# Experts that start with one pair's gather, and half of the memory's products behind the first up products

## The chip, the cores and the metric

The kernel runs as one program on 1 core of one Trainium2 chip. The metric is the device time of an execution in microseconds (us). Five engines work side by side: TensorE (PE; its weight loads are PEld), VectorE (DVE), ScalarE (ACT), GpSimd (POOL) and SyncE (SP), which issues most of the DMA transfers.

## The reference

Two blocks run one after the other on 256 tokens of 1024 features, in float32. The change lies in the first block's two layers. Each is an attention mixer, a layer norm and a mixture of 16 experts, of which a token takes two:

```python
scores = sigmoid(h @ router_w)                      # 256 x 16
# the group of four experts with the best sum of two; in it the best two
gates = sel / sum(sel);  dense_gates = one_hot(idx) weighted by gates
for e in range(16):
    a = silu(h @ w_gate[e]) * (h @ w_up[e])         # 1024 -> 512
    y = y + dense_gates[:, e:e+1] * (a @ w_down[e]) # 512 -> 1024
h = layer_norm(ALPHA * h + y)
```

The second block attends to a memory of 256 rows. Its keys and values, `rms_norm(mem) @ mem_wkv` (1024 to 2048 columns), depend on the input alone. The kernel computes them in four pieces of 512 columns, two in each expert stage of the first block, and keeps them in DRAM until the second block.

## The kernel before

**The expert stage.** The kernel doesn't run each expert on all 256 tokens. It counts for every token its place among the at most 64 (CAP) tokens of an expert, writes these places as matrices of ones and zeros (`pm`, one per tile of 128 tokens, tile name `gv`) and gathers the tokens by matmuls with them. Experts run in eight pairs, each expert of a pair on 64 columns of TensorE. Per pair come gate products, up products, silu times up times gate weight (`act`), a transpose (`tr`), down products and the scatter back to the rows of `res`. `gather(g)` (L1273) makes the transposed inputs of two pairs at once, with 256 columns; the pairs' inputs lie in slots m0 and m1.

**Ahead of the experts.** `LayerNorm.tile` (L206) normalises a tile of 128 tokens, transposes it (L560) and copies it (L564, L566); for the second tile it also splits both tiles into a high and a low float32r part (`split`, L491) for the gather. Then come the routing (L1189 to L1232), the counts by matmul (L1237 to L1241), the places (L1248), `gather(0)`, the memory's products of 512 columns (`memory_gemm`, L1709: 16 matmuls, of 1024 x 512 weights in two halves), which the scheduler fits between the others, and the products that bring the gate weights to the places (L1296). A float32 matmul shows as two records on TensorE, a float32r matmul as one.

**What sets the order.** The functions write the instructions in an order; a scheduler then orders each engine by priority and readiness, and `after` ties an instruction behind another on its engine. Each engine runs its list in that fixed order, and an instruction that waits holds up all behind it. PSUM banks come from rings: `mm` has 3, `acca` and `accb` 2 each, `tp` 1. The small tiles `prob` have 2 buffers: the memory's products are scaled into them (L1734) and sent to DRAM by GpSimd's queue (L1736), and `act` (L1324, L1325) takes the same two.

**The weights' stream.** `plan` (L330) lists the weights as units of 1 MB in the order of use. `Stream` loads them strictly in that order on SP's queue (L141), into 7 buffers called stage and 6 called piece; four units of the first pairs (`slots`) go into main slots that are free then (m4, xl, m1, xh). A unit's load is issued when the oldest buffer of its ring has been given back by `release`, which `gate_or_up` and `down` call after every half (2 MB). A unit's index decides the ring.

Of the kernel before, what the change touches and what calls it, by code (L numbers as in the profile page):

```python
# [16 lines left out]
P = 128  # L17
# [6 lines left out]
NSTAGE = 7  # L24
# [174 lines left out]
class LayerNorm:  # L199
# [6 lines left out]
    def tile(self, t):  # L206
        k = self.k
        self.sqrt, self.last = k.ln_full(self.res, t, self.gb)
        if self.plain:
            if t == 0:  # L210
                self.n = k.slot(self.tags[0]).rearrange("p (j n) -> p j n", j=8)
            self.copied = k.plain_t(self.res[:, t, :], t, self.n)
            if t == 0:
                return

            self.hh = k.slot("m5", F32R).rearrange("p (t j f) -> p t j f", t=2, j=8)
            self.hl = k.slot("m2", F32R).rearrange("p (t j f) -> p t j f", t=2, j=8)
            with k.after(self.sqrt, self.last):
                for i in range(2):
                    v = self.res[:, i, :].rearrange("p (f j) -> p j f", j=8)  # L220
                    k.split(v, self.hh[:, i], self.hl[:, i])
        else:
            if t == 0:
                self.hi, self.lo = k.xt(self.tags[0]), k.xt(self.tags[1])
            self.copied = k.x_t(self.res[:, t, :], t, self.hi, self.lo, self.g)
            if t == 0:
                self.half = self.copied
            self.moved = k.moved
# [38 lines left out]
class Kern:  # L267
# [62 lines left out]
    def plan(self):  # L330
        I, ws = self.I, self.ws
        for l in range(2):
# [31 lines left out]
            def mem(c0):  # L364
                for j0 in (0, 4):
                    ws.raw("mem", w_mem[:, j0:j0 + 4, c0:c0 + 512], 4, 512, j0 // 4)

            mem(1024 * l)
            n = 0
            for k in range(9):  # L370
# [3 lines left out]
                if k > 0:  # L374
                    todo += [("down", e, j0) for j0 in (0, 4) for e in (2 * k - 2, 2 * k - 1)]
                for key in todo:
# [3 lines left out]
                    ws.raw(key[0], *w_ap(*key), n % (NSTAGE + NPIECE) % 2)  # L380
                    n += 1
                    if n == NSTAGE + NPIECE - 2:
                        early("down", 1, 0)
                        early("down", 0, 4)
            mem(1024 * l + 512)
# [793 lines left out]
    def moe(self, l, res, ln):  # L1179
# [6 lines left out]
        for t in range(2):  # L1186
            o = p[:, 16 * t:16 * t + 16]
            for j in range(8):
                nc.tensor.matmul(o, n[:, j, t * P:(t + 1) * P], self.rw[:, j, :], start=(j == 0), stop=(j == 7))  # L1189
# [56 lines left out]
        for e0, e1 in ((0, 4), (4, 16)):  # L1246
            for t in range(2):
                at_pm = nc.vector.tensor_tensor(  # L1248
# [3 lines left out]
                    op=OP.is_equal)  # L1252
        pos = self.sm(48, "gpos")
# [35 lines left out]
        gather(0)  # L1289
        self.memory_gemm(l, 0, [self.prob()[:, 0:512] for t in range(2)], {7: [at_pp]})  # L1290

        p = self.tp()
        gsl = self.sm(8, "gsl")
        for pr in range(8):
            for t in range(2):
                nc.tensor.matmul(p[:, 2 * pr:2 * pr + 2], pm[t][:, P * pr:P * pr + P].bitcast(F32),  # L1296
                                 gates[:, 16 * t + 2 * pr:16 * t + 2 * pr + 2], start=(t == 0), stop=(t == 1))
        pv = p[:, 0:16].rearrange("p (a k) -> p a k", k=2)
        for k in range(2):
            nc.vector.tensor_copy(gsl[64 * k:64 * k + 64, :], pv[64 * k:64 * k + 64, :, k])  # L1300
# [71 lines left out]
        for pr in range(9):  # L1372
# [23 lines left out]
            if pr < 8:  # L1396
                ua = gate_or_up("up", pr)
            if pend is not None:
# [310 lines left out]
    def memory_gemm(self, k, b, out, after={}, mid=None, pair=None):  # L1709

        acc = [self.acc(pair), self.acc(pair)]
        x = self.mem_t.rearrange("p (j n) -> p j n", j=8)
        with ExitStack() as order:
            for j in range(8):
# [11 lines left out]
        if not mid:  # L1726
# [548 lines left out]
```

## Time and profile before

| | |
|---|---|
| median of 3 runs | 1941.78 us (1941.69 to 1943.78) |
| the profiled execution | 1940.31 us, of it 1938.5 us from the first to the last instruction |
| mean granted TensorE clock | 0.998 |
| busy share: PE, PEld, DVE, ACT, POOL | 98%, 75%, 58%, 45%, 2% |
| bytes moved by DMA | 453.36 MB, 234 GB/s over the span |
| first layer's experts | about 150 to 407 us |
| second layer's experts | about 532 to 789 us |

The expert stages are the stretches in which the DMA engines move the most, some 425 GB/s; in most of the rest they move 110 to 240 GB/s. Matmul ends are modelled, so a TensorE that is called busy may still be waiting for pieces of a pipeline; gaps and the distance from one start to the next are the better measure. What ended a gap stands in brackets behind a row.

### The profile page before, as it was taken

Reading aid. Unit: us, or ns where it says so; the run is one execution under the profiler, and the core shown is the slowest. Engines: PE = TensorE matmul, PEld = TensorE weight load, DVE = VectorE, ACT = ScalarE, POOL = GpSimd, SP = SyncE. Lnnn points to the kernel's source line nnn. Section 1 sums busy time; section 2 is a strip of 40 time slices with the busy share of each in tenths; the row PEclk is TensorE's granted clock in tenths of the full one; section 3 lists DMA queues with packets and bytes.
Section 4 is the critical chain, followed back from the end, with each engine's and each line's share of the span. In section 5 each row is a group of like instructions: output and inputs, shape, how many; then the busy total and the mean of one; then the engine's idle time right before and its main releaser. Section 6 shows DMA issues by size and latency. Waiting matters only on the chain.

```text
span 1938.5 us, 27919 instructions
## 1 busy us (share of the span) xinstructions
PE 1891.8 (98%) x11029; PEld 1449.2 (75%) x11029; DVE 1117.4 (58%) x2226; ACT 862.8 (45%) x1550; POOL 46.4 (2%) x93
## 2 busy tenths in 40 slices
PE   6999999999999999999999999999999999999999
PEld 6775444378754443799988988899899986788998
DVE  6875122277741223765579857555655568766554
ACT  5662111056521101654477656544644466656443
POOL 1010000000000000000001000000000000000000
PEclk9999999999999999999999999999999999999999
DMA  8568999964679999655553553555555553434550
GB/s 284 174 232 297 399 426 426 423 235 157 236 305 414 425 426 422 235 187 211 181 185 110 175 217 131 194 179 183 195 174 196 195 164 135 152 109 157 192 196 23
DMA packets 175211, 453.36 MB, mean 234 GB/s; under 512 B 10288, under 2 KB 106012, under 8 KB 148316
## 3 DMA queue, kind: packets, MB, share of 16 engines
q1 hardware_dynamic: 171212, 435.53, 60.2%
q0 software_dynamic: 3856, 15.91, 2.4%
q8 instruction: 91, 1.49, 0.3%
q14 instruction: 52, 0.43, 0.1%
HBM read 446.17 MB, written 5.24 MB: 233 GB/s over the span
## 4 chain that ended last, share of the span: by engine, by line
PE 60%; ACT 2%; DMA 2%; DVE 2%; issue 0%; POOL 0%; ACTq 0%; SPq 0%
PE mm L1588 8%; PE mm L1589 8%; PE mm L1587 8%; PE acca L487 5%; PE acca L488 5%; PE accb L486 4%; PE accb L487 4%; PE accb L488 4%; PE acca L486 4%; PE mm L1315 2%; DMA piece<-in_exp_w_down_dram 1%; DMA piece<-in_exp_w_gate_dram 1%; PE mm L1851 1%; PE acca L1348 1%; PE accb L1348 1%; PE mm L545 1%
## 5 line engine op out<-in xcount | busy, mean ns | idle before, releaser
L167 DVE TENSOR_TENSOR piece<-stage,piece 128x1024 fp32r<-128x1024 f32 (+3 forms) x439 | 513.5, 1179 | 238.2 <-ACT piece L166 236.6
L166 ACT ACTIVATE piece<-stage 128x1024 fp32r<-128x1024 f32 (+3 forms) x439 | 444.1, 1022 | 335.8 <-PE mm L1589 198.3
L1315 PE MATMUL mm<-stage,m 128*64 128x512 f32 x528 | 225.1, 595 | 2.4 <-DMA stage<-in_exp_w_gate_dram 2.4
L1315 PE MATMUL mm<-piece,m 128*64 128x512 f32 x480 | 213.4, 595 | 2.6 <-DMA piece<-in_exp_w_gate_dram 2.5
L1588 PE MATMUL mm<-m,piece 128*128 128x256 f32 x736 | 206.6, 281 | 0.0
L1587 PE MATMUL mm<-m,piece 128*128 128x256 f32 x736 | 206.2, 280 | 0.0
L1589 PE MATMUL mm<-m,piece 128*128 128x256 f32 x736 | 206.1, 280 | 0.0
L1587 PE MATMUL mm<-xh,piece 128*128 128x256 f32 x576 | 163.1, 283 | 0.0
L1589 PE MATMUL mm<-xh,piece 128*128 128x256 f32 x576 | 163.0, 283 | 0.0
L1588 PE MATMUL mm<-xl,piece 128*128 128x256 f32 x576 | 162.9, 283 | 0.0
L486 PE MATMUL accb<-piece,m 128*128 128x512 f32 (+1 forms) x364 | 143.2, 394 | 1.4 <-DVE res L1670 0.8
L487 PE MATMUL accb<-piece,m 128*128 128x512 f32 (+1 forms) x364 | 144.4, 397 | 0.0
L488 PE MATMUL accb<-piece,m 128*128 128x512 f32 (+1 forms) x364 | 144.2, 396 | 0.0
L1587 PEld LDWEIGHTS mm<-m,piece 128*128 128x128 f32 x736 | 138.4, 188 | 1.9 <-issue 0.3
L1588 PEld LDWEIGHTS mm<-m,piece 128*128 128x128 f32 x736 | 138.2, 188 | 1.6 <-issue 0.2
L1589 PEld LDWEIGHTS mm<-m,piece 128*128 128x128 f32 x736 | 138.7, 189 | 0.2 <-issue 0.2
L486 PE MATMUL acca<-piece,m 128*128 128x512 f32 (+1 forms) x348 | 137.3, 396 | 0.9 <-ACT m L496 0.8
L487 PE MATMUL acca<-piece,m 128*128 128x512 f32 (+1 forms) x348 | 137.8, 396 | 0.0
L488 PE MATMUL acca<-piece,m 128*128 128x512 f32 (+1 forms) x348 | 137.3, 395 | 0.0
L1315 PEld LDWEIGHTS mm<-stage,m 128*64 128x64 f32 x528 | 67.7, 137 | 82.9 <-issue 74.8
L1587 PEld LDWEIGHTS mm<-xh,piece 128*128 128x128 f32 x576 | 110.4, 192 | 1.3
L1588 PEld LDWEIGHTS mm<-xl,piece 128*128 128x128 f32 x576 | 110.4, 192 | 1.2
(572 smaller groups left out, 3480.2 us busy)
## 6 DMA issues: line engine op xcount, KB each, us to landing
stage<-in_ffn_wi_dram SPq DMA_DIRECT2D x88, 1024.0 KB, 5.1
stage<-in_ffn_wo_dram SPq DMA_DIRECT2D x44, 1024.0 KB, 5.1
stage<-in_exp_w_gate_dram SPq DMA_DIRECT2D x34, 1024.0 KB, 12.5
stage<-in_exp_w_down_dram SPq DMA_DIRECT2D x34, 1024.0 KB, 13.0
stage<-in_exp_w_up_dram SPq DMA_DIRECT2D x32, 1024.0 KB, 13.0
piece<-in_exp_w_gate_dram SPq DMA_DIRECT2D x30, 1024.0 KB, 10.6
piece<-in_exp_w_up_dram SPq DMA_DIRECT2D x30, 1024.0 KB, 11.0
piece<-in_exp_w_down_dram SPq DMA_DIRECT2D x24, 1024.0 KB, 19.5
```

The source lines that it names most:

```text
L166: nc.scalar.activation(wh, src, AF.Copy)
L167: nc.vector.tensor_tensor(wl, src, wh.bitcast(F32), op=OP.subtract)
L486: nc.tensor.matmul(out, ah, bh, start=first, stop=False)
L487: nc.tensor.matmul(out, ah, bl, start=False, stop=False)
L488: self.last_mm = nc.tensor.matmul(out, al, bh, start=False, stop=last)
L545: self.moved = nc.tensor.transpose(p[:, k * P:(k + 1) * P], src[:, 4 * q + k:D:8], self.c["ident"])
L1315: mm = nc.tensor.matmul(o[64 * k:64 * k + 64, :], x[:, j, s:s + CAP], w[k][:, jj, :], start=(j == 0), stop=(j == 7))
L1348: prev[:] = [nc.tensor.matmul(y[nb][64 * k:64 * k + 64, :], x[:, f, 64 * k:64 * k + 64], w[k][:, cc, nb * 512:(nb + 1) * 512], start=(f == ...
L1587: nc.tensor.matmul(out, wh[:, j, :], hi[:, j, :], start=(j == 0), stop=False)
L1588: nc.tensor.matmul(out, wh[:, j, :], lo[:, j, :], start=False, stop=False)
L1589: nc.tensor.matmul(out, wl[:, j, :], hi[:, j, :], start=False, stop=(j == 7))
L1851: nc.tensor.matmul(po[:, k * P:(k + 1) * P], v[:, mc, h * 256 + cc * P:h * 256 + (cc + 1) * P], pt[t][:, (2 * h + mc) * P:(2 * h + mc + 1) ...
```

## The change

It does five things. (1) The places are written for the first pair alone, then for the rest, behind the copies of the first gather. (2) The gather of the first two pairs is cut in two gathers of 128 columns; the second stands behind the first up products. (3) Of the memory's 16 products the first 8 stay ahead of the experts, and the 8 with the second half of the weights stand behind the second pair's gather; so does the product that brings the gate weights to the places. (4) In the stream, the second half of the memory's weights moves behind the first pair's up weights. (5) The split of the second tile into two parts stands behind that tile's copies.

```diff
--- before.py
+++ after.py
@@ -218,7 +218,8 @@
             with k.after(self.sqrt, self.last):
                 for i in range(2):
                     v = self.res[:, i, :].rearrange("p (f j) -> p j f", j=8)
-                    k.split(v, self.hh[:, i], self.hl[:, i])
+                    with k.after(*(self.copied if i else ())):
+                        k.split(v, self.hh[:, i], self.hl[:, i])
         else:
             if t == 0:
                 self.hi, self.lo = k.xt(self.tags[0]), k.xt(self.tags[1])
@@ -361,11 +362,10 @@
             self.plan_rows("w_out", I["w_out"][l].rearrange("(c p) n -> p c n", p=P), 8)
             early("up", 0, 4)
             w_mem = I["mem_wkv_2"].rearrange("(p j) n -> p j n", j=8)
-            def mem(c0):
-                for j0 in (0, 4):
-                    ws.raw("mem", w_mem[:, j0:j0 + 4, c0:c0 + 512], 4, 512, j0 // 4)
-
-            mem(1024 * l)
+            def mem(c0, j0, ring):
+                ws.raw("mem", w_mem[:, j0:j0 + 4, c0:c0 + 512], 4, 512, ring)
+
+            mem(1024 * l, 0, 0)
             n = 0
             for k in range(9):
                 todo = []
@@ -373,16 +373,23 @@
                     todo += [(name, e, j0) for name in ("gate", "up") for j0 in (0, 4) for e in (2 * k, 2 * k + 1)]
                 if k > 0:
                     todo += [("down", e, j0) for j0 in (0, 4) for e in (2 * k - 2, 2 * k - 1)]
+                if k == 0:
+                    todo.append("mem")
                 for key in todo:
                     if key in slots:
                         ws.use(key[0], held[key])
                         continue
-                    ws.raw(key[0], *w_ap(*key), n % (NSTAGE + NPIECE) % 2)
+                    ring = n % (NSTAGE + NPIECE) % 2
+                    if key == "mem":
+                        mem(1024 * l, 4, ring)
+                    else:
+                        ws.raw(key[0], *w_ap(*key), ring)
                     n += 1
-                    if n == NSTAGE + NPIECE - 2:
+                    if n == NSTAGE + NPIECE - 1:
                         early("down", 1, 0)
                         early("down", 0, 4)
-            mem(1024 * l + 512)
+            for j0 in (0, 4):
+                mem(1024 * l + 512, j0, j0 // 4)
 
             if l == 0:
                 w = I["w_in"][1].rearrange("(p j) n -> p j n", j=8)
@@ -1186,7 +1193,7 @@
         for t in range(2):
             o = p[:, 16 * t:16 * t + 16]
             for j in range(8):
-                nc.tensor.matmul(o, n[:, j, t * P:(t + 1) * P], self.rw[:, j, :], start=(j == 0), stop=(j == 7))
+                routed = nc.tensor.matmul(o, n[:, j, t * P:(t + 1) * P], self.rw[:, j, :], start=(j == 0), stop=(j == 7))
         ws.free.append("xh")
         with self.tc.issue_after(ln.sqrt.ins):
             self.table(AF.Sigmoid)
@@ -1243,13 +1250,17 @@
         nc.vector.scalar_tensor_tensor(posx, sel, -FAR, pp[:, 0:32], op0=OP.mult, op1=OP.add)
 
         pm = [self.mp.tile([P, D], F32R, name="gv", tag="gv", bufs=2) for t in range(2)]
-        for e0, e1 in ((0, 4), (4, 16)):
+
+        def places(e0, e1):
             for t in range(2):
-                at_pm = nc.vector.tensor_tensor(
+                at = nc.vector.tensor_tensor(
                     pm[t][:, CAP * e0:CAP * e1].rearrange("p (e n) -> p e n", n=CAP),
                     c["slot"][:, None, 0:CAP].to_broadcast([P, e1 - e0, CAP]),
                     posx[:, 16 * t + e0:16 * t + e1].rearrange("p (e o) -> p e o", o=1).to_broadcast([P, e1 - e0, CAP]),
                     op=OP.is_equal)
+            return at
+
+        at_pm = places(0, 2)
         pos = self.sm(48, "gpos")
         nc.vector.tensor_copy(pos, pp[:, 0:48])
 
@@ -1286,18 +1297,41 @@
                 nc.scalar.activation(x[:, j0, :], p[:, 0:256], AF.Copy)
                 nc.vector.tensor_copy(x[:, j0 + 1, :], p[:, 256:512])
 
-        gather(0)
-        self.memory_gemm(l, 0, [self.prob()[:, 0:512] for t in range(2)], {7: [at_pp]})
-
-        p = self.tp()
+        def gather_pair(q):
+
+            if not xg:
+                xg.append(self.slot("m0").rearrange("p (j n) -> p j n", j=8))
+            x = xg[0][:, :, P * q:P * q + P]
+            for j0 in range(0, 8, 4):
+                p = self.mm()
+                for j in range(j0, j0 + 4):
+                    o = p[:, P * (j - j0):P * (j - j0) + P]
+                    for t in range(2):
+                        m = pm[t][:, P * q:P * q + P]
+                        nc.tensor.matmul(o, hh[:, t, j, :], m, start=(t == 0), stop=False)
+                        nc.tensor.matmul(o, hl[:, t, j, :], m, start=False, stop=(t == 1))
+                p4 = p.rearrange("p (j n) -> p j n", j=4)
+                nc.scalar.activation(x[:, j0:j0 + 2, :], p4[:, 0:2], AF.Copy)
+                at = nc.vector.tensor_copy(x[:, j0 + 2:j0 + 4, :], p4[:, 2:4])
+            return at
+
+        at_x = gather_pair(0)
+        with self.after(at_x):
+            at_pm = places(2, 16)
+        mem_out = [self.prob()[:, 0:512] for t in range(2)]
+        self.memory_gemm(l, 0, mem_out, {2: [routed], 3: [at_pp]}, js=range(4))
         gsl = self.sm(8, "gsl")
-        for pr in range(8):
-            for t in range(2):
-                nc.tensor.matmul(p[:, 2 * pr:2 * pr + 2], pm[t][:, P * pr:P * pr + P].bitcast(F32),
-                                 gates[:, 16 * t + 2 * pr:16 * t + 2 * pr + 2], start=(t == 0), stop=(t == 1))
-        pv = p[:, 0:16].rearrange("p (a k) -> p a k", k=2)
-        for k in range(2):
-            nc.vector.tensor_copy(gsl[64 * k:64 * k + 64, :], pv[64 * k:64 * k + 64, :, k])
+
+        def place_gates():
+
+            p = self.tp()
+            for pr in range(8):
+                for t in range(2):
+                    nc.tensor.matmul(p[:, 2 * pr:2 * pr + 2], pm[t][:, P * pr:P * pr + P].bitcast(F32),
+                                     gates[:, 16 * t + 2 * pr:16 * t + 2 * pr + 2], start=(t == 0), stop=(t == 1))
+            pv = p[:, 0:16].rearrange("p (a k) -> p a k", k=2)
+            for k in range(2):
+                nc.vector.tensor_copy(gsl[64 * k:64 * k + 64, :], pv[64 * k:64 * k + 64, :, k])
 
         act_t, ptr = [], []
 
@@ -1395,6 +1429,11 @@
                     scatter(pr - 2, y)
             if pr < 8:
                 ua = gate_or_up("up", pr)
+            if pr == 0:
+                with self.after(state["up"]):
+                    gather_pair(1)
+                    place_gates()
+                    self.memory_gemm(l, 0, mem_out, js=range(4, 8), acc=self.mem_out[2])
             if pend is not None:
                 y = down(pr - 1, at)
             if pr == 1:
@@ -1706,12 +1745,12 @@
         self.mem_t = self.slot(tag)
         self.nc.gpsimd.dma_start(self.mem_t, self.memT)
 
-    def memory_gemm(self, k, b, out, after={}, mid=None, pair=None):
-
-        acc = [self.acc(pair), self.acc(pair)]
+    def memory_gemm(self, k, b, out, after={}, mid=None, pair=None, js=range(8), acc=None):
+
+        acc = acc or [self.acc(pair), self.acc(pair)]
         x = self.mem_t.rearrange("p (j n) -> p j n", j=8)
         with ExitStack() as order:
-            for j in range(8):
+            for j in js:
                 if j == 4 and mid:
                     order.enter_context(self.after(mid(at)))
                 if j in after:
@@ -1723,7 +1762,7 @@
                 if j % 4 == 3:
                     self.ws.release()
         self.mem_out = (k, b, acc, out)
-        if not mid:
+        if not mid and j == 7:
             self.memory_out()
         return at
 
```

On TensorE, in the first layer, from the second tile's transposes to the first gate products (`res` to `mm` are the transposes, `tp<-rw,xh` the routing, `tp<-gsel` the counts, `acca` the memory's products, `mm<-gv` the gather, `tp<-ggate` the gate weights). Before:

```order
L1722 MATMUL acca<-stage,m_1438 128x512 x4
L560 MATMUL mm<-ident,res 128x128 x8
L1722 MATMUL acca<-stage,m_1438 128x512
L1189 MATMUL tp<-rw,xh 128x16 x4
L1722 MATMUL acca<-piece,m_1438 128x512
L1189 MATMUL tp<-rw,xh 128x16 x4
L1722 MATMUL acca<-piece,m_1438 128x512 x4
L1237 MATMUL tp<-gsel,blob 128x16
...
L1284 MATMUL mm<-gv,m_1665 128x256
...
L1722 MATMUL acca<-piece,m_1438 128x512 x2
L1296 MATMUL tp<-ggate,gv 128x2 x16
```

And now:

```order
L1761 MATMUL acca<-stage,m_1438 128x512
L567 MATMUL mm<-ident,res 128x128 x8
L1196 MATMUL tp<-rw,xh 128x16 x8
L1761 MATMUL acca<-stage,m_1438 128x512 x2
L1244 MATMUL tp<-gsel,blob 128x16
...
L1311 MATMUL mm<-gv,m_1665 128x128
...
L1761 MATMUL acca<-stage,m_1438 128x512
L1349 MATMUL mm<-stage,m_1744 64x512
```

Between transposes and counts two of the memory's products are left of six, the gather has 128 columns, and the first gate products follow it without the gate weights.

On TensorE again, from the first pair's last up products to its transposes (L1331, now L1365). Before:

```order
L1315 MATMUL mm<-stage,m_1746 64x512
L683 MATMUL tp<-ident,w_1900 128x84
L1315 MATMUL mm<-piece,m_1746 64x512
...
L689 MATMUL tp<-ident,w_1900 128x8
...
L1331 MATMUL tp<-ident,prob 128x128 x4
```

And now:

```order
L1349 MATMUL mm<-stage,m_1744 64x512
L1311 MATMUL mm<-gv,m_1665 128x128
...
L1330 MATMUL tp<-ggate,gv 128x2 x16
L1761 MATMUL acca<-piece,m_1438 128x512
L1311 MATMUL mm<-gv,m_1665 128x128
...
L1761 MATMUL acca<-piece,m_1438 128x512 x7
L690 MATMUL tp<-ident,w_1932 128x84
...
L1365 MATMUL tp<-ident,prob 128x128 x4
```

The second gather, the gate weights and eight products stand between the first pair's up products and the second pair's gate products, which follow L690.

On VectorE, from the second tile's normalisation to the first operations of the routing. Before:

```order
L581 SCALAR_TENSOR_TENSOR res<-res,lnr,gv 128x1024
L493 TENSOR_TENSOR m<-res,m 128x1024 x2
L564 COPY xh<-mm 128x4x128
L1195 TENSOR_TENSOR gbi<-gsc,rb 128x32
L1203 TENSOR_TENSOR gps<-gbi 128x8x3
```

And now:

```order
L588 SCALAR_TENSOR_TENSOR res<-res,lnr,gv 128x1024
L500 TENSOR_TENSOR m<-res,m 128x1024
L571 COPY xh<-mm 128x4x128
L500 TENSOR_TENSOR m<-res,m 128x1024
L1202 TENSOR_TENSOR gbi<-gsc,rb 128x32
L1210 TENSOR_TENSOR gps<-gbi 128x8x3
```

The copy that the routing needs has moved ahead of the second tile's split, and that split now stands directly ahead of the routing.

## Rows read from the trace of the kernel before

**Rows 1.** By stretch: us; PE, PEld, DVE, ACT, POOL; clock; DMA share; GB/s

```profile
150.00:234.00 84.00, 84.00 (x434) 43.35 (x434) 28.40 (x70) 17.78 (x28) 3.21 (x6) 1.00 0.88 347
234.00:236.00 2.00, 2.00 (x12) 0.67 (x10) 0.00 (x0) 0.00 (x0) 0.00 (x0) 1.00 0.73 172
236.00:330.00 94.00, 92.73 (x456) 39.36 (x454) 21.17 (x35) 9.64 (x19) 3.89 (x9) 1.00 1.01 425
```

**Rows 2.** Timeline of SP's queue: start, us, queue, line, operation

```profile
233.71 0.33 SPq L141 DMA_DIRECT2D piece<-in_exp_w_up_dram  x1
```

**Rows 3.** Timeline of TensorE, last pair; in brackets idle before, releaser

```profile
349.08 0.64 PE L1315 MATMUL mm<-stage,m 128*64 128x512 f32 x1 [1.20 <-DMA stage<-in_exp_w_gate_dram]
```

**Rows 4.** Timeline of TensorE, first layer, ahead of the experts and first pair

```profile
155.37 3.68 PE L1722 MATMUL acca<-stage,m 128*128 128x512 f32 x8
158.89 1.05 PE L560 MATMUL mm<-ident,res 128*128 128x128 f32 x8
...
162.38 0.96 PE L1189 MATMUL tp<-rw,xh 128*128 128x16 f32 x8
...
166.71 0.29 PE L1237 MATMUL tp<-gsel,blob 128*128 128x16 f32 x2
...
168.63 0.39 PE L1284 MATMUL mm<-gv,m 128*128 128x256 f32 x1
...
174.29 3.63 PE L1296 MATMUL tp<-ggate,gv 128*128 128x2 f32 x32
177.85 0.64 PE L1315 MATMUL mm<-stage,m 128*64 128x512 f32 x1
...
191.74 0.29 PE L683 MATMUL tp<-ident,w 84*128 84x84 f32 x1
```

**Rows 5.** Timeline of ScalarE, the same stretch: second tile's split and copy

```profile
157.41 2.07 ACT L492 ACTIVATE m<-res 128x1024 fp32r<-128x1024 f32 x1
159.53 0.60 ACT L566 ACTIVATE xh<-mm 128x512 f32<-128x512 f32 x1
```

**Rows 6.** Timeline of VectorE, the same stretch, and the first pair's activation

```profile
157.07 2.02 DVE L493 TENSOR_TENSOR m<-res,m 128x1024 fp32r<-128x1024 f32 x1
...
161.44 0.68 DVE L564 COPY xh<-mm 128x512 f32<-128x512 f32 x1
163.61 0.19 DVE L1195 TENSOR_TENSOR gbi<-gsc,rb 128x32 f32<-128x32 f32 x1 [1.50 <-ACT gsc L1193]
...
166.12 0.19 DVE L1232 SCALAR_TENSOR_TENSOR gsel<-grk,ggrp 128x32 f32<-128x32 f32 x1
...
191.92 0.75 DVE L1325 SCALAR_TENSOR_TENSOR prob<-mm,gsl,prob 128x512 f32<-128x512 f32 x1 [13.62 <-PE mm L1315]
```

**Rows 7.** TensorE at 128 columns: one timeline row; one group: busy us, mean ns

```profile
226.32 1.94 PE L1388 MATMUL mm<-ident,gv 128*128 128x128 f32 x16
...
L1851 PE MATMUL mm<-m,m 128*128 128x128 f32 x128 | 15.2, 277 | 0.1
```

**Rows 8.** Timeline of ScalarE, first pair's activation

```profile
185.04 1.28 ACT L1324 ACT_TABLE_LOAD   x1 [9.87 <-PE mm L1315]
186.34 0.60 ACT L1324 ACTIVATE prob<-mm 128x512 f32<-128x512 f32 x1
```

**Rows 9.** Issue of the memory's result on GpSimd's queue, and its landing

```profile
174.62 0.54 POOL L1736 DMA_DIRECT2D memKV<-prob  x1 [6.38 <-ACT prob L1734]
...
DMA to landing us min/median/max: 6.3/6.5/6.7
```

**Rows 10.** Timeline of TensorE: first pair's transposes, behind the second pair's gates

```profile
200.13 0.75 PE L1331 MATMUL tp<-ident,prob 128*128 128x128 f32 x4
```

**Rows 11.** Second block: a gap of TensorE; then two stretches as in rows 1

```profile
1636.13 1.22 PE L1132 MATMUL mm<-ident,prob 128*128 128x128 f32 x6 [2.53 <-DVE prob L1999]
...
1637.00:1644.00 7.00, 6.25 (x24) 4.45 (x23) 5.35 (x16) 3.27 (x11) 0.00 (x0) 0.51 0.38 117
1644.00:1646.00 2.00, 1.80 (x16) 1.21 (x15) 0.56 (x1) 1.16 (x3) 0.00 (x0) 1.00 0.98 399
```

## The prediction

> **What bounds the kernel now.** I read the page first: TensorE is busy 98% of a span of 1938.5 us, so a change pays only if it takes work or waiting off TensorE, or moves whatever TensorE waits for. Then busy time by stretch for the first layer's experts. From 150 us, where the memory's products begin, to 234 us, in the third pair, TensorE is busy in all 84.00 of 84.00 us; from 236 to 330 us the DMA engines are busy throughout (share 1.01, 425 GB/s) and TensorE has its first gaps [rows 1]. So the stage has two limits, one after the other. Early on the 13 buffers of weights are full and a load can start only when TensorE gives a buffer back: in 234 to 236 us the rate drops to 172 GB/s [rows 1], because the queue had run dry and its next issue, at 233.71 us, waited for the first half of the third pair's up products [rows 2]. After that issue the loads never pause, and at the end of the stage TensorE waits for them, 1.20 us before a gate of the last pair [rows 3]. So the end of the stage lies a fixed stretch of loading behind 233.71 us. What decides is when TensorE reaches that half: it must first have done all that stands ahead of it, whatever the order.
>
> **The change, part by part.** I follow the first layer and carry it to the second, whose program repeats it.
>
> *The head.* Before, gathers start at 168.63 us and gates at 177.85 us [rows 4]. What now fills TensorE between the normalisation of the second tile and the first gate is half as many products of the memory: 8 records (3.68 us at 155.37, so 0.44 each) go from ahead of the second tile's transposes down to 2, and in the whole head 16 records leave [rows 4].
> The transposes wait for the tile: VectorE's next operation starts at 157.07 [rows 6], so they start at about 157.2, not 158.89. ScalarE's copy follows 0.64 us later as before (158.89 to 159.53), at 157.85 to 158.45, and its split, 2.07 us, now behind it, ends at 160.5 [rows 4, 5]. VectorE: split of the first tile 157.07 to 159.1, copy 159.1 to 159.8; its split of the second tile needs ScalarE's and runs 160.5 to 162.5 [rows 6]. The routing's first operation came 2.17 us behind the copy's start (161.44 to 163.61), which would be 161.3, but the split stands ahead of it in VectorE's order: 162.5. That is 1.1 us sooner than 163.61, so the selection, 2.70 us later (166.12 plus 0.19), is ready at 165.2 [rows 6].
> TensorE has by then nothing left: routing records until 160.7 (0.96 us for eight [rows 4]), two products of 0.88 us until 162.5, then an idle 2.7 us. The counting matmuls run at 165.2 and one product behind them ends at 167.1 (both together took 1.92 us, 166.71 to 168.63 [rows 4]); the smaller places, 128 columns for 256, are ready a little before. So the gather starts at 167.1.
>
> *The gather of a pair.* 32 matmuls as before, each with 128 moving columns instead of 256. No row of before has this precision at 128 columns. The nearest is a transpose with 128 columns behind a 128-column weight load: 16 in 1.94 us, the last one 0.27 long, so 0.11 us apart [rows 7]. Before, the gather took 168.63 to 174.29 less four product records of 0.44, or 3.9 us, 0.12 each [rows 4]. Hence 32 x 0.11 = 3.5 us: the gather of one pair costs nearly what that of two did, and both pairs together cost 3.1 us more. Ends: 1.9 us if the time follows the columns, and 7.6 us if such a matmul runs as the two full-precision records of a 128-column product do (15.2 us / 128 = 0.119 each, so 0.238 [rows 7]). I take 3.5, the transposes' row, since both load as many weights per matmul.
> The Trainium skill ("TensorE: Matmul & The Clock Gate", section Back-to-back issue gap) gives 134 cycles for 128 columns, an estimate of 56 ns, by which a gather would take 1.8 us and the sum over both layers would be 6.8 us smaller; the same page's section on LDWEIGHTS puts a load at its columns over 1.2, an estimate of 107 ns for 128. The 0.11 us of rows 7 agrees with the second and not with the first.
>
> *First gate.* Gather 167.1 to 170.6, one product to 171.5: the gates begin 6.4 us sooner than 177.85. Everything else of the head is only moved.
>
> *Behind the first up products.* Gate and up of the first pair take 13.9 us (177.85 to 191.74), then come the second pair's gather 3.5, the 32 records of the gates' places 3.6 (174.29 to 177.85) and 16 records of the memory's products 7.0 [rows 4]: 171.5 + 13.9 + 3.5 + 3.6 + 7.0 = 199.5 us, where the second pair's gates stood at 191.74. **7.7 us late.** As a check: idle in the head about 1.0 + 0.4 + 2.7 us (ahead of the transposes, ahead of the routing, ahead of the counts), plus 3.1 us for the gathers, the rest rounding.
>
> *The loads meanwhile.* The queue can go on 6.4 us sooner, but one buffer of 13 now holds the memory's second half, so 1 MB more is still to load: 1.0486 MB at 425 GB/s, 2.5 us [rows 1]. Gates and up free seven buffers; the eighth in turn is the memory's, given back at 199.5. Seven loads from 175 on last 17.3 us, so the queue stands dry for some 5 us before 199.5. All that it gained is lost, and TensorE's place decides again.
>
> *A new wait.* The two result buffers into which the memory's halves are scaled are the ones that the first pair's activation takes next. ScalarE's table load and silu therefore wait for a transfer that used to be over long before: silu ran 174.62 + 6.5 us of landing against 185.04 [rows 8, 9]. Now the products end at M = 199.5; issue M + 0.33 (174.29 to 174.62), landing 6.5, table 1.28, silu 0.60, VectorE's product 0.75, 0.15 of hops: M + 9.6 [rows 4, 6, 8, 9]. Queued behind it on TensorE are the first pair's transposes, which stand between the second pair's gates and up, and all up products behind them. In the first layer the gates and two small transposes last 8.4 us (191.74 to 200.13 [rows 4, 10]): 1.2 us of waiting. In the second there are no small transposes, 16 x 0.43 = 6.9 us: 2.7 us. **Together 3.9 us.** Between 0, if it lands in time, and any delay of the landing one for one.
>
> *The clock.* The one idle of this length in the trace, 2.53 us before a transpose at 1636.13, is followed by a granted clock of 0.51 from 1637 to 1644 us, the lower level of 1.2 GHz, and 1.00 from 1644 on [rows 11]. The head's idle of 2.7 us stands at that edge. If the clock falls as there, a microsecond after work resumes and for nearly 7, one product costs 0.9 us more, 23 gather matmuls run 0.11 us slower each: 3.3 us with rounding. I take it in one of the two layers: 3.3 us; ends 0 and 6.6.
> The Trainium skill ("TensorE: Matmul & The Clock Gate", section HAM oscillation) says that a wait ahead of a burst makes the burst start at half clock, so it counts against this change in both layers, 6.6 us; rows 11 agree for one place, and a second such place this trace does not have.
>
> **The sum.** 2 x 7.7 + 3.9 + 3.3 = 22.6 us. What the stage loses is not regained: its end hangs on the loads, which are as late as TensorE at the third pair. The profiled execution took 1940.31 us (1.8 around its span), 1.5 below the median of 1941.78: 1940.31 + 22.6 + 1.5 = 1964.4. I say **1964**.
>
> **Rivals.**
> - *The loads' restart decides* (faster). Freed buffers come 6.4 us sooner, 2.5 go to the extra MB: 3.9 us a layer, 7.8 in all, 1934. It would need a queue that never runs dry before 234 us; the dip there and the issue on TensorE's release [rows 1, 2] speak against it.
> - *Half-rate gathers.* 7.6 us a gather: 4.1 more, four times, 16.4: 1980. For it: every matmul of this precision in the trace has 256 columns or more, so no row excludes it.
> - *Cheap gathers, no clock fall.* 1.6 us less, four times, and 3.3: 1954.5; with the landing in time as well, 3.9 less, 1951.
> - *No change.* The late TensorE would have to be made good by its waits for weights at the end, but the loads are late by as much, so little can come from there. I leave it what lies between the first and third rival.
>
> **Chances.** Forecast 0.52 (1957 to 1970), half-rate gathers 0.24, cheap gathers 0.15, faster 0.05, no change 0.04. Range 1951 to 1980, from the cheap end to the dear one. What a measurement can tell from no change is about 0.2%, 4 us: faster 0.05, same 0.04, slower 0.91.
>
> **What would show it.** First gates near 171.5 us, after an idle of 2 to 3 us ahead of the counting matmuls; gather matmuls 0.11 us apart; second pair's gates near 199.5; a dry queue before that; transposes waiting on VectorE's product behind a late table load; the first half of the third pair's up products some 9 us after 233.7, and loads without a pause from there on. It is wrong if that half is reached at the old time or sooner, if the queue still has freed buffers when TensorE gets there, or if gathers at 128 columns are not 0.11 us apart.

## The result and the profile after

| | before | after |
|---|---|---|
| median | 1942.03 us (1941.69 to 1943.78, 4 runs) | 1987.22 us (1985.47 to 1991.78, 4 runs) |
| span of the profiled execution | 1938.5 us | 1983.7 us |
| mean granted TensorE clock | 0.998 | 0.981 |

The changed kernel is slower: ratio 1.0234, 95% interval 1.0221 to 1.0247. That is 45 us, where 22.6 had been forecast. The direction was right; the size came out twice the forecast.

The second layer of the program stands 382.10 us behind the first (first gates 559.95 against 177.85 before), and after the change 24.03 us more, by which the first stage ends later. Less 406.13, the second layer's places in the changed kernel compare with the first's:

| | before | forecast | after, layer 1 | after, layer 2 |
|---|---|---|---|---|
| first gates | 177.85 | 171.5 | 177.39 | 175.68 |
| second pair's gates | 191.96 | 199.5 | 212.40 | 209.83 |
| first pair's transposes (layer 2 before: 198.60) | 200.13 | 209.0 | 223.31 | 220.48 |
| end of the stage, later by | | 8.9 and 10.4, without the clock | 24.03 | 21.79 |

The forecast for the transposes is 200.13 + 7.7 + 1.2 and 198.60 + 7.7 + 2.7.

All of the loss is there when TensorE reaches the first pair's transposes (23.2 and 21.9 us), and the stage ends as late as that. Against the forecast for the transposes 14.3 and 11.5 us are missing; less the 3.3 that the forecast gave the clock in one layer that is 22.5, the whole miss.

TensorE of the changed kernel (the lines of [rows 4], now L567, L1196, L1244, L1311, L1330, L1349 and L1761; in brackets idle before and what ended it):

```profile
156.66 1.16 PE L567 MATMUL mm<-ident,res 128*128 128x128 f32 x8 [0.73 <-DVE res L588]
158.06 2.24 PE L1196 MATMUL tp<-rw,xh 128*128 128x16 f32 x16 [0.23 <-ACT xh L573]
160.15 3.15 PE L1761 MATMUL acca<-stage,m 128*128 128x512 f32 x4
164.75 0.58 PE L1244 MATMUL tp<-gsel,blob 128*128 128x16 f32 x2 [1.46 <-DVE gsel L1239]
...
167.94 1.09 PE L1311 MATMUL mm<-gv,m 128*128 128x128 f32 x1
...
174.17 0.41 PE L1311 MATMUL mm<-gv,m 128*128 128x128 f32 x1
174.38 0.41 PE L1312 MATMUL mm<-gv,m 128*128 128x128 f32 x1
...
177.39 0.85 PE L1349 MATMUL mm<-stage,m 128*64 128x512 f32 x1
...
191.87 0.28 PE L1312 MATMUL mm<-gv,m 128*128 128x128 f32 x1
191.98 0.27 PE L1311 MATMUL mm<-gv,m 128*128 128x128 f32 x1
...
193.32 5.47 PE L1330 MATMUL tp<-ggate,gv 128*128 128x2 f32 x32
...
203.81 8.59 PE L1761 MATMUL acca<-piece,m 128*128 128x512 f32 x14
212.24 0.24 PE L690 MATMUL tp<-ident,w 84*128 84x84 f32 x1
...
223.31 0.75 PE L1365 MATMUL tp<-ident,prob 128*128 128x128 f32 x4 [2.67 <-DVE prob L1359]
...
300.35 1.94 PE L1349 MATMUL mm<-stage,m 128*64 128x512 f32 x2 [6.07 <-DMA stage<-in_exp_w_down_dram]
```

The wait of 6.07 us for weights at 300 us (6.0 in the second layer) is new, but it costs the end 0.8 us at most: the stage was 23.2 us late before it and is 24.0 us late behind it. The same matmul of 128 columns starts 0.21 us behind the last at 174 us and 0.11 us at 192 us. What differs is the clock. By stretch (columns as in [rows 1]), first layer, then second:

```profile
152.00:160.90 8.90, 7.83 (x47) 5.73 (x47) 7.88 (x13) 6.49 (x7) 0.00 (x0) 0.99 1.00 403
160.90:177.90 17.00, 15.54 (x51) 10.77 (x51) 7.47 (x33) 0.77 (x2) 2.12 (x4) 0.50 0.29 73
177.90:194.90 17.00, 17.00 (x95) 7.63 (x91) 0.75 (x2) 0.38 (x1) 0.00 (x0) 1.00 0.92 358
194.90:208.30 13.40, 13.40 (x43) 9.79 (x44) 1.08 (x4) 0.38 (x1) 0.00 (x0) 0.50 0.41 173
...
567.00:570.30 3.30, 3.30 (x4) 0.80 (x3) 3.27 (x13) 0.18 (x1) 0.00 (x0) 0.50 0.72 226
570.30:573.80 3.50, 2.50 (x17) 1.95 (x17) 2.38 (x16) 0.00 (x0) 0.00 (x0) 0.99 0.35 145
573.80:584.00 10.20, 10.20 (x38) 7.27 (x39) 3.00 (x5) 0.77 (x2) 0.00 (x0) 0.50 0.12 25
584.00:601.00 17.00, 17.00 (x98) 8.16 (x94) 0.00 (x0) 0.38 (x1) 0.00 (x0) 1.00 0.90 365
601.00:611.20 10.20, 10.20 (x34) 7.62 (x34) 1.08 (x4) 0.38 (x1) 0.00 (x0) 0.50 0.46 192
```

That is 54 us at 0.50, the lower level of 1.2 GHz, where [rows 1] show 1.00 in the first layer's. (The clock is at 0.50 for 6.8 us more in each layer, around the 6 us waits for weights, where the loads set the pace.) The fall at 160.9 comes before the idle time ahead of the counts, and the one at 194.9 with no idle time at all: TensorE is busy in 17.00 of the 17.00 us ahead of it.

ScalarE's table load, which answers to [rows 8]:

```profile
220.58 1.28 ACT L1358 ACT_TABLE_LOAD   x1 [7.46 <-DMA memKV<-prob]
```

The issue of the memory's result on GpSimd's queue, as in [rows 9]:

```profile
212.56 0.54 POOL L1775 DMA_DIRECT2D memKV<-prob  x1 [46.03 <-ACT prob L1773]
```

SP's queue, which answers to [rows 2]:

```profile
191.59 0.33 SPq L141 DMA_DIRECT2D stage<-in_exp_w_gate_dram  x1
212.43 0.33 SPq L141 DMA_DIRECT2D piece<-in_exp_w_gate_dram  x1
...
256.90 0.33 SPq L141 DMA_DIRECT2D stage<-in_exp_w_up_dram  x1
```

The table load ahead of the first silu waits for the memory's result to land, as forecast. The queue issues nothing between 191.59 and 212.43 us. 256.90 is the load that the first half of the third pair's up products releases (into the other ring now), 23.2 us later than 233.71.

### The profile page after: what moved, and what is told of

The parts are those of the page before. It is cut to its first block, busy times and chain, and to the rows that moved or that the text cites. A ratio compares the mean times of both kernels' runs of the same rounds, so it can differ in the third digit from the quotient of the medians.

```text
span 1983.7 us, 28053 instructions
## 1 busy us (share of the span) xinstructions
PE 1925.1 (97%) x11093; PEld 1468.8 (74%) x11093; DVE 1117.7 (56%) x2226; ACT 862.9 (43%) x1550; POOL 46.2 (2%) x93
## 4 chain that ended last, share of the span: by engine, by line
PE 83%; DVE 5%; DMA 5%; ACT 4%; issue 3%; SPq 0%; POOL 0%; ACTq 0%; DVEq 0%; POOLq 0%
PE mm L1349 9%; PE mm L1628 8%; PE mm L1626 8%; PE mm L1627 8%; PE accb L493 6%; PE accb L494 6%; PE accb L495 6%; PE acca L495 5%; PE acca L494 5%; PE acca L493 5%; PE acca L1382 2%; DMA stage<-in_exp_w_down_dram 2%; PE accb L1382 2%; PE acca L1088 1%; ACT piece L166 1%
## 5 line engine op out<-in xcount | busy, mean ns | idle before, releaser
L1349 PE MATMUL mm<-stage,m 128*64 128x512 f32 x544 | 231.2, 604 | 12.1 <-DMA stage<-in_exp_w_down_dram 12.1
L1349 PE MATMUL mm<-piece,m 128*64 128x512 f32 x464 | 208.9, 603 | 0.0
L1349 PEld LDWEIGHTS mm<-stage,m 128*64 128x64 f32 x544 | 69.3, 139 | 94.0 <-issue 91.1
## 6 DMA issues: line engine op xcount, KB each, us to landing
piece<-in_exp_w_up_dram SPq DMA_DIRECT2D x28, 1024.0 KB, 10.4
```

The lines of the kernel that those rows point to most:

```text
L1349: mm = nc.tensor.matmul(o[64 * k:64 * k + 64, :], x[:, j, s:s + CAP], w[k][:, jj, :], start=(j == 0), stop=(j == 7))
```

## The experiments

Theory A: the missing 22 us are the clock, lowered by long runs of matmuls with few columns. Theory B: they are transfers and loads that wait for the new stretch. All ratios are to the kernel before.

**e1_weave**

```diff
-                    gather_pair(1)
-                    place_gates()
-                    self.memory_gemm(l, 0, mem_out, js=range(4, 8), acc=self.mem_out[2])
+                    self.weave(weave_gather(1), weave_gates(), self.weave_memory(mem_out))
...
+        for r in range(8):
+            for g, n in ((memory, 1), (gather, 4), (gates, 2)):
```

> The changed kernel, with one edit: behind the first up products, the 8 products of the memory, the 32 matmuls of the second gather and the 16 products that bring the gate weights are dealt out in turn (one product, four gather matmuls, two gate-weight products, eight times over) instead of one kind after the other. Same work, same place. Theory A (the clock): the 22 us that the prediction missed are TensorE at its lower clock, twice a layer, because long runs of matmuls with few columns stand together; dealt out among wide products they no longer lower it, the granted clock stays at 1.00 behind the up products, and the second pair's gates begin 6.8 us sooner in the first layer and some 5 us in the second: about 1975 us. Theory B (the transfers): what costs is the late result of the memory and the loads that stand still until this stretch is over; the order inside the stretch hardly matters: 1984 to 1990 us.

Measured: 1968.49 us (1966.26 to 1970.73), ratio 1.0140 (1.0123 to 1.0156), 18.7 us less than the change. By stretch, first layer:

```profile
160.90:177.90 17.00, 15.11 (x51) 10.63 (x51) 7.47 (x33) 0.77 (x2) 2.12 (x4) 0.51 0.29 71
...
191.60:206.70 15.10, 14.47 (x84) 10.43 (x82) 1.27 (x5) 2.03 (x4) 1.09 (x2) 1.00 0.69 276
```

The clock stays at 1.00 behind the up products, and the same work takes 15.1 us (191.60 to 206.67, the second pair's gates) where it took 20.9. The fall in the head, which the edit doesn't touch, is still there. More is gained than A's 12 us: the memory's products end sooner, and the transposes' wait of 2.67 and 3.56 us is gone in both layers (no idle time ahead of them in the first):

```profile
214.84 0.75 PE L1389 MATMUL tp<-ident,prob 128*128 128x128 f32 x4
```

B is out.

**e2_own_buffers**

```diff
-        mem_out = [self.prob()[:, 0:512] for t in range(2)]
+        mem_out = [self.prob()[:, 0:512], self.mp.tile([P, 512], F32, name="mout", tag="mout", bufs=1)]
```

> The changed kernel, with one edit: the second half of the memory's result is scaled into a buffer of its own, so that the first pair's activation finds a free one and silu no longer waits for the transfer to DRAM. Theory A (the clock): the waits of 2.7 and 3.6 us ahead of the first transposes go, and TensorE is ahead by as much in the third pair: about 6 us less, 1981 us, or nothing where the loads set the end anyway. Theory B (the transfers): this wait also holds the buffers of weights, and the waits of 6 us for weights at 300 and 704 us go with it: 1972 to 1976 us.

Measured: 1981.02 us (1976.23 to 1984.37), ratio 1.0206 (1.0189 to 1.0223), 6.2 less than the change. That is the size of the two waits (2.67 and 3.56 us), as A says. The clock falls in the same stretches, but two of the falls are shorter in the profiled execution, which at 1976.23 us is the fastest of the four. TensorE at the counts of the first layer, and the stretch at 0.50 behind the first up products:

```profile
164.61 0.52 PE L1244 MATMUL tp<-gsel,blob 128*128 128x16 f32 x2 [2.65 <-DVE gsel L1239]
```

```profile
195.40:202.20 6.80, 6.80 (x28) 5.77 (x27) 0.66 (x3) 0.00 (x0) 0.00 (x0) 0.50 0.75 313
```

Here the clock of the first layer's head holds at 1.00 until the 2.65 us of idle time end, and is at 0.50 for 13.7 us from there. Behind the up products it is at 0.50 for 6.8 us, where it was 13.4. So the same matmuls are followed by falls of different length in different executions.

**e3_split_order**

```diff
-                    k.split(v, self.hh[:, i], self.hl[:, i])
+                    with k.after(*(self.copied if i else ())):
+                        k.split(v, self.hh[:, i], self.hl[:, i])
```

> The kernel before, with part 5 of the change alone: the second tile's split behind that tile's copies. Both theories: the selection is ready about 1 us sooner, but TensorE is busy throughout the head, so nothing is gained: 1940 to 1944 us. If this edit alone lowered the clock in the head (routing and counts closer together, with fewer wide products between), 1950 us or more.

Measured: 1942.91 us (1940.87 to 1945.22), ratio 1.0006 (0.9996 to 1.0015). Part 5 alone costs and gains nothing; the clock is 1.00 in the head.

**e4_cut_gather**

```diff
-        gather(0)
+        gather_pair(0)
+        gather_pair(1)
```

> The kernel before, with the cut of the first gather alone: two gathers of 128 columns, both ahead of the experts, everything else in its place. By the prediction's term (0.11 us per matmul of 128 columns against 0.12 of 256) 3.1 us more per layer: 1948 us. Theory A (the clock): 64 matmuls of 128 columns in a row, with no idle time, are such a stretch of few columns, and the clock falls in it: 1955 to 1962 us with a granted clock of 0.50 somewhere between 172 and 185 us. If columns alone set the time of a matmul, no change: 1942 us.

Measured: 1949.44 us (1948.78 to 1951.36), ratio 1.0037 (1.0023 to 1.0052): 7.0 us, near the 6.2 of the prediction's term. The first gates come 3.4 us later than before (177.85), where the term says 3.1 a layer:

```profile
181.23 0.64 PE L1334 MATMUL mm<-stage,m 128*64 128x512 f32 x1
```

By stretch, first layer's gathers and gate weights, then the second layer's gathers, and the stretch from the end of its gate weights on:

```profile
168.60:175.90 7.30, 7.30 (x65) 7.26 (x65) 3.70 (x10) 1.15 (x3) 0.00 (x0) 1.00 0.35 92
177.70:181.20 3.50, 3.50 (x33) 3.50 (x31) 0.00 (x0) 0.69 (x1) 1.09 (x2) 1.00 0.61 150
554.00:563.00 9.00, 9.00 (x71) 8.01 (x70) 3.86 (x10) 2.22 (x5) 0.00 (x0) 1.00 0.15 60
...
565.70:571.70 6.00, 6.00 (x20) 2.89 (x22) 0.33 (x2) 0.00 (x0) 0.00 (x0) 0.50 0.58 210
```

The same 64 narrow matmuls and 32 gate-weight records leave the clock at 1.00 in the first layer and see a fall near their end in the second. A's time (1955 to 1962 us) and its fall between 172 and 185 us did not come. A fall at such a run without idle time did come, in the other layer, so the run alone doesn't decide whether the clock falls.

**e7_fill_alone** and **e5_weave_fill** (the same line, without and with the edit of e1_weave)

```diff
+                for i in range(fill if j == 0 else 0):
+                    self.nc.tensor.matmul(acc[i % 2], x[:, 0, 0:P], w[:, 0, :], start=True, stop=True)
```

> The changed kernel with the 8 extra wide products in the head alone, and the stretch behind the up products as the change left it. Theory A: only the fall in the head goes, the one behind the up products stays (0.50 from about 189 to 202 us): 1987 less 2 x 5.9, 1975 us. Theory B: 1985 to 1990 us.

Measured: 1978.6 us (1978.0 to 1982.66), ratio 1.0186 (1.0170 to 1.0201), 8.6 less than the change with 8 more products a layer: B is out here too. A's 1975 is missed by 3.6 us; it had put no cost on the extra products. The fall in the head is gone, the one behind the up products stays. By stretch, first layer:

```profile
160.00:178.00 18.00, 18.00 (x96) 10.76 (x96) 9.79 (x35) 2.77 (x4) 2.12 (x4) 1.00 0.49 143
...
192.30:202.50 10.20, 10.20 (x34) 7.67 (x34) 1.08 (x4) 0.38 (x1) 0.00 (x0) 0.51 0.43 180
```

TensorE has no idle time in this head (18.00 of 18.00 us busy). So the extra products stand among the narrow matmuls and also fill the waits of 0.73, 0.23 and 1.46 us, and this run doesn't show which of the two keeps the clock up in the head.

> The changed kernel with the dealing out of e1_weave, and with 8 wide matmuls more in the head of each layer (a product of the memory's weights, written to the memory's accumulators before its first real product and overwritten by it: extra work whose result is not used), so that the head before the first gather has as many wide products between its narrow ones as the kernel before. Theory A (the clock): the remaining fall of the clock, from 161 to 178 us, goes too; the first gates begin near 171.5 us, as predicted, in place of 177.4, so 2 x 5.9 us less than e1_weave: 1957 us. That is also the prediction's sum without its clock term and without its silu term (1942 + 15.4). Theory B (the head's length is set by the order of VectorE and by idle time, not by the clock): the extra products cost time or nothing, 1966 to 1974 us.

Measured: 1960.96 us (1960.86 to 1962.42), ratio 1.0098 (1.0082 to 1.0113), 26.3 less than the change; the two edits alone gave 18.7 and 8.6. A's 1957 is missed by 4 us. By stretch: the first layer, in it the dry queue, and the second layer:

```profile
150.00:206.00 56.00, 55.38 (x280) 31.77 (x280) 20.35 (x56) 11.26 (x16) 3.21 (x6) 1.00 0.73 268
197.00:201.50 4.50, 4.50 (x26) 3.07 (x25) 0.00 (x0) 0.69 (x1) 0.54 (x1) 1.00 0.02 7
532.00:620.00 88.00, 87.11 (x436) 49.34 (x435) 30.14 (x72) 15.76 (x23) 1.10 (x2) 1.00 0.80 309
```

Its TensorE, first gates and second pair's gates:

```profile
174.21 0.64 PE L1373 MATMUL mm<-stage,m 128*64 128x512 f32 x1
...
203.15 0.64 PE L1373 MATMUL mm<-stage,m 128*64 128x512 f32 x1
```

The clock is 1.00 in both heads. The first gates begin 2.7 us later than the forecast 171.5. I put that down to the extra products (eight of 0.44 us are 3.5), which no run shows apart. Less that the second pair's gates are at 200.4, where 199.5 was forecast, and the time over before is 19.2 - 2 x 2.7 = 13.8 us, where the sum without clock and silu wait said 15.4. The queue is dry for 4.5 us, where 5 were forecast.

**e9_apart**

```diff
                     gather_pair(1)
-                    place_gates()
-                    self.memory_gemm(l, 0, mem_out, js=range(4, 8), acc=self.mem_out[2])
+                with self.after(state["gathered"]):
+                    at = self.memory_gemm(l, 0, mem_out, js=range(4, 8), acc=self.mem_out[2])
+                with self.after(at):
+                    place_gates()
```

> The changed kernel, with one edit in the stretch behind the first up products: the 8 products of the memory (7 us of wide matmuls) stand between the second gather (32 matmuls of 128 columns, 3.5 us) and the gate weights (32 records of 2 columns, 3.6 us) and no longer behind both. Theory A (it is the length of the run of narrow matmuls, 7.1 us where the two stand together): each run alone is too short, the clock stays at 1.00 there, and the second pair's gates begin 5 to 6 us sooner per layer, as in e1_weave; the memory's result leaves 3.6 us sooner as well: 1968 us. If either run alone is enough (in e6_lean 2.4 us of the same gate weights were), the clock falls behind it and the gain is that of the sooner result alone: 1978 to 1982 us.

Measured: 1976.64 us (1972.78 to 1978.07), ratio 1.0180 (1.0164 to 1.0195). By stretch, first layer: gather, its end and what follows, products, gate weights, behind them:

```profile
190.00:193.50 3.50, 2.57 (x24) 2.43 (x23) 0.42 (x1) 0.38 (x1) 0.00 (x0) 1.00 1.02 431
193.50:196.50 3.00, 3.00 (x12) 2.27 (x11) 0.42 (x1) 0.38 (x1) 0.00 (x0) 0.53 1.02 426
196.50:203.00 6.50, 6.50 (x17) 2.85 (x15) 0.00 (x0) 0.69 (x1) 0.00 (x0) 0.95 0.29 121
203.00:206.50 3.50, 3.50 (x33) 3.50 (x31) 0.00 (x0) 0.69 (x1) 1.09 (x2) 1.00 0.61 147
206.50:211.00 4.50, 4.50 (x13) 1.27 (x14) 0.74 (x4) 0.83 (x1) 0.00 (x0) 0.62 0.65 237
```

A's 1968 did not come: in either run alone the clock falls at its end or right behind it, in both layers. The gather has 0.9 us of idle time in it, which could have its part in that fall; the gate weights have none. So a run of 3.6 us can be enough, and the length of the joined run isn't needed. The wait for silu is gone in both layers, as the range for this case has it. The time is a little under that range; the falls are short: in the rows above the clock is 0.53 over 3.00 us and 0.62 over 4.50, where the change has 0.50 over 13.40.

**e6_lean** and **e8_lean_spread**: the kernel before, with narrow matmuls moved behind the third pair's gates

```diff
-        for pr in range(8):
+        place_gates(0, 3)
...
-                for q in range(0, 8, 2):
+                turn(0)
+            if pr in (3, 4, 5):
+                with self.after(state["gate"]):
+                    turn(2 * pr - 4)
...
+            if pr == 2:
+                with self.after(state["up"]):
+                    place_gates(3, 8)
```

> The kernel before, with the gate weights of pairs 3 to 7 (20 of 32 records, 2.3 us) and the transposes of the places of pairs 2 to 7 (12 of 16, 1.4 us) moved behind the third pair's gates and up products. Nothing else is changed, and nothing of the change under study is in it. It tests the part of the prediction that says what bounds a stage: its end lies a fixed stretch of loading behind the third pair's first up half. By that TensorE gets there 2.3 + 1.4 = 3.7 us sooner in each layer, and the moved work finds room in the 5 us in which TensorE waits for weights later: 1935 us, the issue of 233.71 us at about 230. If instead TensorE's own work sets the end (it is busy 98%), the moved work costs the same later: 1940 to 1943 us.

Measured: 1936.76 us (1934.64 to 1939.99), ratio 0.9971 (0.9960 to 0.9983): faster than both kernels. SP's queue, the issue of [rows 2], then TensorE's clock around the moved gate weights:

```profile
231.37 0.33 SPq L141 DMA_DIRECT2D piece<-in_exp_w_up_dram  x1
```

```profile
234.70:237.10 2.40, 2.40 (x24) 2.38 (x24) 0.75 (x1) 0.00 (x0) 0.00 (x0) 1.00 0.99 406
237.10:241.30 4.20, 4.20 (x14) 1.19 (x15) 0.32 (x2) 0.00 (x0) 0.00 (x0) 0.61 1.02 425
```

The issue comes 2.3 us sooner, where 3.7 had been expected, and in the profiled execution the stages are 1.8 and 1.0 us shorter. 2.4 us of gate weights were enough for a fall here; 3.6 us of them were not in [rows 4].

In e8_lean_spread the gate weights of a pair stand in that pair: `if 2 < pr < 8: place_gates(pr, pr + 1)`.

> As e6_lean (the kernel before, with gate weights and transposes of the places moved behind the third pair's gates), but the moved matmuls stand apart: the gate weights of each pair from the fourth on in that pair (4 records, 0.45 us), 8 of the 16 transposes where they were, 4 in the fourth pair and 4 in the fifth. In e6_lean the clock fell to 0.50 for some 3.5 us right behind the 20 gate-weight records (238 to 241 us, and 617 to 620 us), though no idle time stood ahead of it, and the scatter waited 0.7 us for a copy. Theory A (long runs of narrow matmuls lower the clock): both falls go, 1.7 us each, and the wait; 1.0 us of transposes comes back ahead of the third pair: 1933 us. Theory B (the fall in e6_lean has another cause, such as the idle time of the scatter 10 us earlier): the falls stay, 1936 to 1938 us.

Measured: 1936.64 us (1934.67 to 1937.12), ratio 0.9967 (0.9955 to 0.9979), no better than e6_lean. That misses A's 1933 and lies in B's range, but the falls went as A says. Both are gone (first row below, where 0.61 stood), and the first stage ends 3.4 us sooner than before. The second is 0.6 us longer than before in this execution; in it stand a wait that the profile gives no cause for and a fall around its end (second row):

```profile
234.30:241.20 6.90, 6.90 (x34) 2.30 (x32) 0.75 (x1) 0.60 (x1) 0.00 (x0) 1.00 1.00 417
```

```profile
648.16 1.01 PE L1352 MATMUL acca<-piece,m 128*64 128x512 f32 x1 [4.13 <-issue]
```

## Why the prediction fell short

**Right: the structure.** TensorE decides, its place at the third pair sets the loads, and the stage's end is as late as that (23.2 us at the issue, 24.0 at the end; in e6_lean it moves the other way). The loads' restart did not make it faster: the queue ran dry, as said. (The 5 us for that are 7.2 by the prediction's own figures, 175 + 17.3 against 199.5; the sum doesn't use them.)

**Right: the sizes at full clock.** Gather matmuls 0.11 us apart (second gather), 3.1 us a layer for the cut gather (e4_cut_gather, 7.0 us for both), the second pair's gates within 1 us of 199.5 once the clock is kept and the 2.7 us of the extra products are taken off (e5_weave_fill). Half-rate gathers, the rival at 1980 us, come nearest to the time and fit the first gather's 7.5 us, but not for the rival's reason: the second gather starts at 0.11 us. The 56 ns that the prediction takes from the Trainium skill ("TensorE: Matmul & The Clock Gate", section Back-to-back issue gap) are given there for a matmul by itself, without the load of its weights; they are not its figure for a gather, which loads weights for every matmul.

**Right, a little small: the silu wait.** 2.67 and 3.56 us for 1.2 and 2.7; e2_own_buffers takes 6.2 us off. The order of events was as forecast; the landing was the term that was too small. The result was issued at 212.56 us and the table load began at 220.58. The landings took 7.7 to 8.0 us in the first layer and 7.4 to 7.6 in the second, where 6.5 had been taken from [rows 9].

**Wrong: the clock.** The step that failed is "I take it in one of the two layers: 3.3 us; ends 0 and 6.6." It went wrong in three ways.
- *Its cause.* It took [rows 11], one fall behind 2.53 us of idle, for the condition, and looked for idle time of that length. In the changed kernel the clock is down at 160.9 us, before that idle time, behind 0.73 and 0.23 us of it, eight transposes and 16 routing records of 16 columns. Extra wide products there keep it up (e7_fill_alone), but they fill the idle time too. In e2_own_buffers, whose head is the same, the first layer's clock does fall behind the idle time that the prediction feared (2.65 us), so in the head the cause is not shown. The Trainium skill ("TensorE: Matmul & The Clock Gate", section HAM oscillation) explains such falls by waits ahead of a burst; [rows 11] agree, and so does e2_own_buffers with its 2.65 us; the fall at 194.9 us does not, since TensorE never waited there.
- *Its places.* Nothing was said of the stretch behind the up products, where 3.5 us of gather and 3.6 us of gate weights were put back to back. The narrow work was priced at full clock, and whether it would keep the clock was not asked.
- *Its length.* Nearly 7 us once, from [rows 11], against 17.0 and 13.4 us in the first layer and 3.3, 10.2 and 10.2 in the second.

In the first layer the head cost 5.9 us more than forecast (177.39 against 171.5), the stretch behind the up products 6.8 (20.9 against 14.1), the silu wait 1.5; in the second layer 4.2, 1.1 in the gates that follow, 5.1 and 0.9. That is the 14.3 and 11.5 us above, within 0.3. Less the silu wait that leaves 23 us, where the prediction had 3.3 for the clock. The range was too narrow for the same reason: 6.6 us was set as the end of a term that nothing in the trace bounded from above.

**Open:** what lowers the clock in the one case and not in the other. Shown is that most of the missing time is the lower clock, and that behind the up products dealing the same work out keeps the clock up, in both layers (e1_weave, e5_weave_fill). A rule for narrow matmuls is not shown. Runs of 2.4 to 7 us saw a fall in the places above, but not in e4_cut_gather's first layer, nor in e7_fill_alone's first gather, nor in [rows 4], nor elsewhere in the kernel before. In its second block, 44 records of 128 columns run without a gap, then one of 512 and 32 more of 128:

```profile
1174.40:1179.40 5.00, 5.00 (x46) 4.96 (x44) 4.28 (x7) 2.40 (x7) 0.00 (x0) 1.00 0.01 3
1179.40:1184.10 4.70, 4.63 (x37) 4.25 (x36) 4.70 (x7) 1.37 (x3) 0.00 (x0) 1.00 0.20 31
```

The clock stays at 1.00 through all of it.

## What to carry to other kernels

When work is moved, look at what is left together: a run of matmuls with few columns, or a head that has lost its wide products, went with half clock here in many places, though not in all, and the profile called TensorE busy there. Deal narrow matmuls out among wide ones, and price a moved stretch at both clocks, even where rows show the same run at full clock: the 32 gate-weight records kept it in [rows 4] and were followed by a fall in e9_apart. Where loads hang on the place that TensorE has reached, move narrow work behind that place.

## What the runs showed of the hardware

- The clock fell with TensorE busy in 17.00 of 17.00 us (194.9 us), so idle time is not needed.
- A matmul of 128 columns behind a load of 128 weight columns starts 0.11 us behind the last at clock 1.00 and 0.21 at 0.50: the pair takes nearly twice as long as a whole. The gate weights (2 columns) took 3.63 us [rows 4] and 5.47 where the clock fell inside them.
- The same instructions can see a fall in one layer and none in the other (e4_cut_gather).
- Some 76 records of 128 columns with one of 512 among them left the clock at 1.00 (kernel before, 1174 to 1184 us), so a run of narrow matmuls is not enough for a fall.
- The same transfer of the memory's result landed after 6.5 us in the kernel before [rows 9] and after 7.7 to 8.0 us in the changed kernel's first layer.
